# Four layers of a diffusion trunk on one core: queue order from a recorder, and one transpose for each word of q, k and P

## The chip, the core and the metric

The kernel runs on one core of a Trainium2 chip. The core has a matrix engine (TensorE, PE in the profile, with its weight loads as PEld), a vector engine (VectorE, DVE), a scalar engine (ScalarE, ACT), GpSimd (POOL) and SyncE (SP), which issues the transfers between the chip's memory and the core's SBUF. TensorE writes to PSUM, eight banks of 128 x 512 words. Each engine works through its own queue in order and waits at semaphores for the others. The metric is the device time of one execution in microseconds.

## The reference, cut to what matters

One step of a four-layer trunk over 128 context tokens and 256 latent tokens, width 2048, all in f32. Layers 0 and 3 are windowed attention (16 query heads, 4 key heads, head size 128, rotary on latents, a sink a head), layer 1 is neighbourhood attention on a 4 x 64 grid (16 heads, a relative bias), layer 2 is a gated MLP with 128 x 128 mixing of positions.

```python
for i in range(DEPTH):                       # kinds: win, nat, gmlp, win
    sh, sc, gt = split(silu(cond) @ w_ada[i] + b_ada[i])
    h = rmsnorm(x, norm_g[i]) * (1 + sc) + sh
    q, k, v, z = split(h @ w_in)             # q, k normed a head, rotary in win
    s = q @ k.T * d ** -0.5                  # own window and all context keys
    P = softmax([s + mask_or_bias, sink])    # nat: no sink
    x = x + gt * ((P @ v * silu(z)) @ w_out)
# gmlp: u, v = gelu(h @ w_in); o = u * (w_s @ layernorm(v) + b_s) * silu(z)
```

Context tokens read context tokens alone; latents read their own window or neighbourhood and 128 cached context keys. The results are the new x of both sequences and the new keys and values of the context.

## The kernel before, in words

All 384 tokens go through each layer together; x is kept transposed, 16 blocks of 128 features by 384 tokens. TensorE has no exact f32 product in one pass, so a number is split in two fp32r words, high and low (H = the rounded number, L = number - H; `split`, one ACT copy and one VectorE subtraction), and a product is three matmuls, high x high, high x low, low x high (`mm3`, `a_unit`, `b_unit`). Weights come in pieces of 128 x 1024 words (0.5 MB): SP loads one into one of four `raw` slots, `prep` splits it into one of three H and L slots, and TensorE uses it for one unit of 24 main matmuls, of 384 columns (`a_unit`, weights stationary) or 512 (`b_unit`, h stationary). `take` asks for the pieces some units ahead.

The order of every queue is written out by hand, in the order of the Python program. Between two units, `bg` advances what runs beside the projections by one step: `step_heads` (the attention heads, generators that yield where a result must come back), `step_misc` (generators for q, k, v, caches), `step_conv` (splits of the gated output) and `step_ada` (rows of the next layer's modulation on VectorE). Some of these decide by an own running count of time for TensorE, VectorE and ACT (`pe_t`, `dve_t`, `act_t`, added to in `mm`, `trR`, `_v`, `act`).

Where transposes stand: `k_gen` (four k blocks in the neighbourhood layer, one in each window layer) norms and rotates k with tokens on partitions, splits it in SBUF into two buffers pH and pL, transposes 12 blocks of 128 x 128 of each to PSUM by `trR` (line 118, fp32r words against an fp32r identity), and copies them out by `ev` (ACT or VectorE, whichever its count says is free first). `q_gen` norms and splits q of four heads likewise; `head` then transposes three blocks of each word, computes the scores, takes the maximum and exponentials into Pt, writes 1/sum x Pt as high word PH (ACT) and low word PLT (VectorE), transposes seven blocks of each word, and computes P @ v. A head so comes to TensorE for q, scores, the two words of P, and the output.

Lines of the profile are those of helpers: L109 is every matmul, L118 every transpose, L122 `tensor_tensor` on VectorE, L133 `scalar_tensor_tensor`, L129 `tensor_scalar`, L150 every ACT instruction, L142 VectorE's copies, L137 the modulation's products. So groups are told apart by their tiles: `hH`, `hL` are the words of h, `H`, `L` of a weight piece, `bk` a PSUM bank, `identR` marks the transposes, `aux,pair` the gMLP's mixing. A matmul is shown as out<-moving,stationary.

Of the kernel before, what the change touches and what calls it, by code (L numbers as in the profile page):

```python
# [1 line left out]

# [5 lines left out]
F32 = mybir.dt.float32  # L8
# [6 lines left out]
P = 128  # L15
# [21 lines left out]
    return bass.AP(ap.tensor, ap.offset, a)  # L37


class Net:  # L40
    def __init__(self, tc, pool, psum, dram, a):
        self.tc, self.nc, self.a = tc, tc.nc, a
        self.pe_t = self.dve_t = self.act_t = self.slot_t = 0.0
        self.lr = {}

# [67 lines left out]
        self.mm(out, aH, bL, False, False)  # L113
        self.mm(out, aL, bH, False, stop)

    def trR(self, out, in_):
        self.pe_t += 0.057
        self.nc.tensor.transpose(out.bitcast(F32R), in_, self.identR)  # L118

    def vtt(self, out, in0, in1, op):  # L120
        self._v(self._n(out) / 960 + 0.07)
# [311 lines left out]
    def setup(self):  # L433
        nc, a = self.nc, self.a
        self.scratch()
        craw, th = self.arow[:, :32], self.arow[:, 32:64]
        self.dma(craw, a["cT"])
        for i in range(NXP):
            self.xt[i] = self.new(f"pair{NPAIR + i}", 1536)
            self.dma(self.xt[i], a["xT"][:, i * 1536:(i + 1) * 1536])  # L440
        self.dma_upto(10)
        nc.scalar.dma_start(self.sel, a["sel"])
        self.act(th, craw, AF.Tanh, scale=0.5)
        make_identity(nc, self.ident)
# [254 lines left out]
    def k_gen(self, kind, li, grp, pi):  # L699
# [10 lines left out]
        for t in range(3):  # L710
# [14 lines left out]
                self.dma(dst[:, n:n + 512], pr[:, :512])  # L725
            else:
                yield
        hi, lo = self.palloc("x", F32R), self.palloc("x", F32R)
        pH, pL = hi[1], lo[1]
        if kind == "win":  # L730
            c3 = pr[:, :512].rearrange("p (h d) -> p h d", h=4)
            self.vtt(c3, c3, _bcast(self.gq, 1, 4), ALU.mult)
        for t in (1, 2, 0):
            o = slice(t * 512, (t + 1) * 512)
            self.split(pH[:, o], pL[:, o], pr[:, o])
        yield
        self.prel(pi)
        kH, kL = self.palloc("m", F32R), self.palloc("m", F32R)
        if kind == "win":
            self.ck = self.new("ck", 1024, F32R)  # L740
        for part, (dst, src) in enumerate(((kH, pH), (kL, pL))):
            dv = dst[1]
            for m in range(3):
                bank = self.abank()
                for i in range(4):
                    if kind == "nat":
                        h, t = divmod(m * 4 + i, 3)
                    else:
                        h, t = divmod(m * 4 + i, 2) if m < 2 else (i, -1)
                        t += 1  # L750
                    self.trR(bank[:, i * P:(i + 1) * P], src[:, t * 512 + h * P:t * 512 + h * P + P])
                if kind == "nat":
                    self.ev(dv[:, m * 512:(m + 1) * 512], bank)
                elif m < 2:
                    self.ev(dv.rearrange("p (h x) -> p h x", h=4)[:, 2 * m:2 * m + 2, :256],
                            bank.rearrange("p (h x) -> p h x", h=2))
                else:
                    self.ev(self.ck[:, part * 512:(part + 1) * 512], bank)
            yield
        self.prel(hi)  # L760
        self.prel(lo)
        grp["k"] = (kH, kL)

    def v_block(self, bk3, kind, li, grp):
# [18 lines left out]
    def q_gen(self, kind, li, grp, pi):  # L783
        pr = pi[1]
        st, st2, st3 = self.stat(), self.stat(), grp["cq"]
        yield
        self.squares(pr, st, 0, 8)
        if kind == "win":
            self.rope(pr[:, 512:1024], self.aux[:, :P], self.aux[:, 256:256 + P])
        yield  # L790
        self.squares(pr, st, 8, 12)
        if kind == "win":
            self.rope(pr[:, 1024:1536], self.aux[:, P:256], self.aux[:, 256 + P:512])
        self.vts(st2, st, P * EPS, None, ALU.add)
# [6 lines left out]
        if grp["n"] == 3:  # L801
            self.px.sort(reverse=True)
        hi, lo = self.palloc("x", F32R), self.palloc("x" if grp["n"] < 3 else "m", F32R)
        pH, pL = hi[1], lo[1]
        for t in range(3):
            o = slice(t * 512, (t + 1) * 512)
            self.split(pH[:, o], pL[:, o], pr[:, o])
        self.prel(pi)
        yield
        grp["q"] = (hi, lo)  # L810

    def head(self, kind, li, h, grp, kvg, zz):

        hh = h % 4
        kv = h // 4 if kind == "win" else hh
        qs, kT, V = ([i[1] for i in g] for g in (grp["q"], kvg["k"], kvg["v"]))
        sm = self.sm[h % 2]
        mx, nm, rs, es, rr, tt = (sm[:, 4 * i:4 * i + 3] for i in range(6))
        for part in range(2):
            bank = self.abank()  # L820
            for t in range(3):
                self.trR(bank[:, t * P:(t + 1) * P], qs[part][:, t * 512 + hh * P:t * 512 + hh * P + P])
            self.ev(self.qT[:, part * T:(part + 1) * T], bank[:, :T])
        if hh == 3:
            for i in grp["q"]:
                self.prel(i)
        yield
        b0, b1 = self.abank(), self.abank()
        k3 = [k[:, kv * T:(kv + 1) * T] for k in kT]
# [3 lines left out]
        for t, b, o in ((0, b0, P), (1, b1, 0)):  # L833
# [13 lines left out]
        Pt = self.new("Pt", 896)  # L847
# [33 lines left out]
        pt = []  # L881
        for part, src in enumerate((pH, pL)):
            b0, b1 = self.abank(), self.abank()
            for kc in range(3):
                for t in range(2):
                    o = kc * 256 + t * P
                    b, o = (b0, o) if o < 512 else (b1, o - 512)
                    s = P + t * T + kc * P
                    self.trR(b[:, o:o + P], src[:, s:s + P])
            self.trR(b1[:, 256:T], src[:, :P])  # L890
            pt.append(self.new("PLT" if part else "PTH", 896, F32R))
            self.ev(pt[part][:, :512], b0)
            self.ev(pt[part][:, 512:896], b1[:, :T])
            yield
# [486 lines left out]
    def run(self):  # L1381
# [3 lines left out]
        for l in range(4):  # L1385
# [124 lines left out]
```

## Time and profile before

| | |
|---|---|
| Median of 3 runs | 3072.14 us (3071.66 to 3074.43) |
| The profiled execution | 3072.06 us, span 3070.2 us |
| Mean granted TensorE clock | 0.998 |
| PE, PEld busy | 3032.9 us (99%), 2771.4 us (90%) |
| DVE, ACT busy | 2174.0 us (71%), 1271.6 us (41%) |
| Moved by DMA | 599 MB, mean 195 GB/s |

A busy share of PE counts matmuls from a start to a modelled end; they are pipelined, and the spans of successive ones overlap. The distance from one start to the next is the time that a matmul takes out of the stream. [...]

### The profile page before, as it was taken

Reading aid. Unit: us, or ns where it says so; the run is one execution under the profiler, and the core shown is the slowest. Engines: PE = TensorE matmul, PEld = TensorE weight load, DVE = VectorE, ACT = ScalarE, POOL = GpSimd, SP = SyncE. Lnnn points to the kernel's source line nnn. Section 1 sums busy time; section 2 is a strip of 40 time slices with the busy share of each in tenths; the row PEclk is TensorE's granted clock in tenths of the full one; section 3 lists DMA queues with packets and bytes.
Section 4 is the critical chain, followed back from the end, with each engine's and each line's share of the span. In section 5 each row is a group of like instructions: output and inputs, shape, how many; then the busy total and the mean of one; then the engine's idle time right before and its main releaser. Section 6 shows DMA issues by size and latency. Waiting matters only on the chain.

```text
span 3070.2 us, 45356 instructions
## 1 busy us (share of the span) xinstructions
PE 3032.9 (99%) x17616; PEld 2771.4 (90%) x17616; DVE 2174.0 (71%) x3604; ACT 1271.6 (41%) x2322; POOL 51.7 (2%) x29
## 2 busy tenths in 40 slices
PE   7999999999999999999999999999999999999999
PEld 4788899978989898998888999999999998999999
DVE  4478789868788888887988998445355566455654
ACT  4355555354444545534333222222232335455542
POOL 0000000000000000000000000000000000000000
PEclk9999999999999999999999999999999999999999
DMA  9756555976666666677777676444454474333343
GB/s 385 276 192 213 200 165 176 337 252 212 206 205 206 204 214 200 205 243 269 246 242 248 219 254 213 132 131 127 134 165 125 135 251 145 114 103 104 106 128 124
DMA packets 187361, 599.05 MB, mean 195 GB/s; under 512 B 21764, under 2 KB 47620, under 8 KB 187140
## 3 DMA queue, kind: packets, MB, share of 16 engines
q1 hardware_dynamic: 186712, 596.00, 58.3%
q8 instruction: 138, 2.26, 0.3%
q14 instruction: 79, 0.65, 0.1%
q10 hardware_dynamic: 432, 0.13, 0.0%
HBM read 580.31 MB, written 15.75 MB: 194 GB/s over the span
## 4 chain that ended last, share of the span: by engine, by line
PE 94%; DVE 2%; ACT 2%; issue 1%; DMA 1%; POOL 0%; SPq 0%; DVEq 0%; ACTq 0%; POOLq 0%
PE bk L109 92%; PE bk L118 3%; ACT junk L150 1%; DVE L L122 1%; DVE pair L133 1%; ACT H L150 0%; DVE pair L122 0%; POOL cq L165 0%; DMA pair<-i_w_ada 0%; ACT Pt L150 0%; DVE junk L137 0%; DMA pair<-i_xT 0%; DMA raw<-i_win_B 0%; DVE PLT L133 0%; DVE Pt L122 0%
## 5 line engine op out<-in xcount | busy, mean ns | idle before, releaser
L150 ACT ACTIVATE H<-raw 128x1024 fp32r<-128x1024 f32 x640 | 676.2, 1058 | 895.1 <-PE bk L109 805.4
L109 PE MATMUL bk<-hH,H 128*128 128x384 f32 x3072 | 1037.5, 338 | 3.4 <-DVE pair L122 3.4
L109 PE MATMUL bk<-hH,L 128*128 128x384 f32 x3072 | 1027.6, 334 | 0.0
L109 PE MATMUL bk<-hL,H 128*128 128x384 f32 x3072 | 1027.0, 334 | 0.0
L122 DVE TENSOR_TENSOR L<-raw,H 128x1024 fp32r<-128x1024 f32 x640 | 781.6, 1222 | 275.8 <-ACT H L150 267.3
L109 PE MATMUL bk<-L,hH 128*128 128x512 f32 x1536 | 600.9, 391 | 8.9 <-DVE L L122 8.9
L109 PE MATMUL bk<-H,hH 128*128 128x512 f32 x1536 | 607.5, 396 | 0.0
L109 PE MATMUL bk<-H,hL 128*128 128x512 f32 x1536 | 602.0, 392 | 0.3 <-DVE hL L122 0.3
L109 PEld LDWEIGHTS bk<-hH,H 128*128 128x128 f32 x3072 | 576.9, 188 | 13.7 <-issue 6.5
L109 PEld LDWEIGHTS bk<-hL,H 128*128 128x128 f32 x3072 | 577.1, 188 | 0.6
L109 PEld LDWEIGHTS bk<-hH,L 128*128 128x128 f32 x3072 | 576.7, 188 | 0.0
L109 PEld LDWEIGHTS bk<-L,hH 128*128 128x128 f32 x1536 | 289.5, 188 | 66.7 <-DVE L L122 11.0
L109 PEld LDWEIGHTS bk<-H,hL 128*128 128x128 f32 x1536 | 289.3, 188 | 65.3 <-DVE hL L122 3.8
L109 PEld LDWEIGHTS bk<-H,hH 128*128 128x128 f32 x1536 | 289.2, 188 | 64.6 <-issue 6.5
L137 DVE CUSTOM_DVE_ANT_0 junk<-araw,cbc,accA 128x1024 bf16<-128x1024 f32 x240 | 307.5, 1281 | 14.2 <-ACT junk L150 7.9
L137 DVE CUSTOM_DVE_ANT_0 junk<-araw,cbc,bada 128x1024 bf16<-128x1024 f32 x240 | 307.5, 1281 | 10.0 <-ACT junk L150 3.0
L133 DVE SCALAR_TENSOR_TENSOR pair<-bk,ada,pair 128x128 f32<-128x128 f32 x320 | 118.6, 413 | 202.4 <-PE bk L109 202.4
L150 ACT ACTIVATE pair<-bk 128x512 f32<-128x512 f32 (+3 forms) x156 | 86.9, 562 | 195.7 <-PE bk L109 172.4
L150 ACT ACTIVATE PLT<-bk 128x512 fp32r<-128x512 f32 (+2 forms) x63 | 34.0, 563 | 168.4 <-PE bk L118 150.2
L150 ACT ACTIVATE PTH<-bk 128x512 fp32r<-128x512 f32 (+2 forms) x74 | 37.0, 523 | 123.1 <-PE bk L118 87.9
L109 PE MATMUL bk<-pair,qT 128*128 128x384 f32 (+2 forms) x336 | 74.9, 332 | 0.0
L150 ACT ACTIVATE junk<-pair 128x128 bf16<-128x128 f32 x216 | 66.8, 309 | 13.4 <-DVE ada L137 5.9
(151 smaller groups left out, 2150.3 us busy)
## 6 DMA issues: line engine op xcount, KB each, us to landing
araw<-i_w_adaT SPq DMA_DIRECT2D x240, 512.0 KB, 3.8
pair<-i_w_ada SPq DMA_DIRECT2D x96, 512.0 KB, 8.2
raw<-i_win_B SPq DMA_DIRECT2D x96, 512.0 KB, 4.2
raw<-i_nat_B SPq DMA_DIRECT2D x96, 512.0 KB, 4.5
raw<-i_win_O SPq DMA_DIRECT2D x64, 512.0 KB, 3.7
raw<-i_gm_V SPq DMA_DIRECT2D x64, 512.0 KB, 4.6
raw<-i_gm_U SPq DMA_DIRECT2D x64, 512.0 KB, 4.5
raw<-i_gm_Z SPq DMA_DIRECT2D x64, 512.0 KB, 4.5
```

Of the source, the lines that this page charges most:

```text
L109: self.nc.tensor.matmul(out, lhsT, rhs, start=start, stop=stop, **kw)
L118: self.nc.tensor.transpose(out.bitcast(F32R), in_, self.identR)
L122: self.nc.vector.tensor_tensor(out=out, in0=in0, in1=in1, op=op)
L133: self.nc.vector.scalar_tensor_tensor(out=out, in0=in0, scalar=s, in1=in1, op0=op0, op1=op1)
L137: self.nc.vector.tensor_tensor_reduce(out=out, in0=in0, in1=in1, op0=op0, op1=op1, scale=1.0, scalar=scalar, accum_out=acc)
L150: self.nc.scalar.activation(out, in_, f, **kw)
```

## The change

Two things are changed. First, `self.nc` is no longer the chip's instruction builder but a recorder (`Rec`). The Python program runs as before and lists its instructions; `add` finds for each what it must come after (data of another instruction, or mere order on its own engine), by tile, column range and the generation of a buffer. `cost` gives each instruction a time on its engine and a time to its result. `in_order` plays the list through in program order on a model of the five queues; `due` works back from TensorE's starts to when each instruction must have started; `schedule` builds a new order, one instruction at a time: TensorE takes the earliest of the program's that is ready, with 250 ns added to results of other engines, and the other queues take what is due first. Main matmuls (those that read h) keep their order among themselves. `order` does this three times, and `emit` issues everything in order of the planned start.

Second, transposes. `trR` is replaced by `tr`, which transposes plain f32 words against the f32 identity. k, q and the scaled P are no longer split in SBUF: each is transposed once, and the split into high and low words is done out of the PSUM bank. P is scaled in place, on ACT or VectorE, and Pt has two buffers (tags Pt and PH) in turn. k's blocks go in three steps of four, with a yield behind each.

```diff
-        self.tc, self.nc, self.a = tc, tc.nc, a
+        self.tc, self.nc, self.a = tc, Rec(tc.nc), a
...
-    def trR(self, out, in_):
-        self.pe_t += 0.057
-        self.nc.tensor.transpose(out.bitcast(F32R), in_, self.identR)
+    def tr(self, out, in_):
+        self.pe_t += 0.084
+        self.nc.tensor.transpose(out, in_, self.ident)
...  k_gen
-        hi, lo = self.palloc("x", F32R), self.palloc("x", F32R)
-        pH, pL = hi[1], lo[1]
...
-        for t in (1, 2, 0):
-            o = slice(t * 512, (t + 1) * 512)
-            self.split(pH[:, o], pL[:, o], pr[:, o])
+        kH, kL = self.palloc("m", F32R), self.palloc("m", F32R)
         yield
+        dH, dL = kH[1], kL[1]
+        for m in range(3):
+            bank = self.abank()
+            for i in range(4):
...
+                self.tr(bank[:, i * P:(i + 1) * P], pr[:, t * 512 + h * P:t * 512 + h * P + P])
+            if kind == "nat":
+                o = slice(m * 512, (m + 1) * 512)
+                self.split(dH[:, o], dL[:, o], bank)
...
+            yield
...  q_gen
-        hi, lo = self.palloc("x", F32R), self.palloc("x" if grp["n"] < 3 else "m", F32R)
-        pH, pL = hi[1], lo[1]
-        for t in range(3):
-            o = slice(t * 512, (t + 1) * 512)
-            self.split(pH[:, o], pL[:, o], pr[:, o])
-        self.prel(pi)
         yield
-        grp["q"] = (hi, lo)
+        grp["q"] = pi
...  head
-        for part in range(2):
-            bank = self.abank()
-            for t in range(3):
-                self.trR(bank[:, t * P:(t + 1) * P], qs[part][:, t * 512 + hh * P:t * 512 + hh * P + P])
-            self.ev(self.qT[:, part * T:(part + 1) * T], bank[:, :T])
+        bank, pr = self.abank(), grp["q"][1]
+        for t in range(3):
+            self.tr(bank[:, t * P:(t + 1) * P], pr[:, t * 512 + hh * P:t * 512 + hh * P + P])
+        self.split(self.qT[:, :T], self.qT[:, T:], bank[:, :T])
...
-        pH, pL = self.new("PH", 896, F32R), self.new("PLT", 896, F32R)
         for t, lo, hi, _ in seg:
-            self.act(pH[:, lo:hi], Pt[:, lo:hi], AF.Identity, scale=rr[:, t:t + 1])
-            self.vstt(pL[:, lo:hi], Pt[:, lo:hi], rr[:, t:t + 1], pH[:, lo:hi].bitcast(F32), ALU.mult, ALU.subtract)
+            if self.act_t <= self.dve_t:
+                self.act(Pt[:, lo:hi], Pt[:, lo:hi], AF.Identity, scale=rr[:, t:t + 1])
+            else:
+                self.vts(Pt[:, lo:hi], Pt[:, lo:hi], rr[:, t:t + 1], None, ALU.mult)
         yield
-        for part, src in enumerate((pH, pL)):
...
+                self.tr(b[:, o:o + P], Pt[:, s:s + P])
+        self.tr(b1[:, 256:T], Pt[:, :P])
+        pt = [self.new("PTH", 896, F32R), self.new("PLT", 896, F32R)]
+        for lo, hi, b in ((0, 512, b0), (512, 896, b1[:, :T])):
+            self.split(pt[0][:, lo:hi], pt[1][:, lo:hi], b)
+        yield
...  run
+        self.nc.emit()
```

The recorder's prices and its planner, cut to their core:

```python
    def cost(self, e, op, a, k):          # ns on the engine, ns to the result
        n = self.cols(a[0] if a else k["out"])
        if e == "tensor":
            if op == "transpose":
                d = 57
            elif "tile_position" in k:
                d = 128
            elif a[2].dtype == F32R:
                d = (n + 32) / 2.4 if n > P else 57
            else:
                d = max(4 * (n + 16) / 2.4, 224)
            return d, d + 190
        if e == "vector":
...
            if op in ("tensor_tensor", "tensor_copy", "bn_stats", "tensor_reduce"):
...
                d = m / 0.96 + 72
...
            return d, d + 90
        if e == "scalar":
...
            d = n / 1.2 + 97 + (75 if hasattr(k.get("scale"), "ap") or hasattr(k.get("bias"), "ap") else 0)
...
            return d, d + 115
        if e == "gpsimd":
            return 650 + 140 * n, 750 + 140 * n
        return 330, 2100
...
    SEM, LDW, LAG = 45, 108, 56
    MARGIN = 250
...
    def schedule(self, late):
...
        key = [float(i) if self.eng[i] == 0 else late[i] for i in range(n)]
...
            i = ready[e][0][1]
            if e == 0:
                if load + self.LDW + self.LAG > t and not self.long[i]:
                    i = min((i for _, i in ready[0] if self.long[i]), default=i)
...
                load = max(load + self.LDW, last)
                t = last = max(t, load + self.LAG)
            if e in (1, 2) and wait[e]:
                end, hold = t + self.dur[i], None
                for est, j in wait[e]:
                    if est < end and late[j] < end and late[j] < late[i] and (hold is None or est < hold):
                        hold = est
                if hold is not None:
                    free[e] = hold
                    continue
...
    def order(self, passes=3):
        start, done = self.in_order()
        for _ in range(passes):
            start, done = self.schedule(self.due(start))
        return sorted(range(len(self.ops)), key=lambda i: (start[i], i))
```

`long` is an instruction of over 100 ns by `cost`, so transposes and matmuls of 128 fp32r columns are short.

## Rows read from the trace of the kernel before

**Rows 1.** The page: each engine's busy us, share, instructions; the chain that ended last.

```profile
PE 3032.9 (99%) x17616; PEld 2771.4 (90%) x17616; DVE 2174.0 (71%) x3604; ACT 1271.6 (41%) x2322; POOL 51.7 (2%) x29
...
PE 94%; DVE 2%; ACT 2%; issue 1%; DMA 1%; POOL 0%; SPq 0%; DVEq 0%; ACTq 0%; POOLq 0%
```

**Rows 2.** Timeline of TensorE, one burst: start, us, line, operation, tiles, count.

```profile
1004.36 0.39 PE L109 MATMUL bk<-L,hH 128*128 128x512 f32 x1
...
1005.27 0.39 PE L109 MATMUL bk<-H,hL 128*128 128x512 f32 x1
1005.50 0.71 PE L118 MATMUL bk<-identR,PH 128*128 128x128 f32 x7
...
1006.35 0.39 PE L109 MATMUL bk<-L,hH 128*128 128x512 f32 x1
```

**Rows 3.** Timeline of TensorE around a burst of the gMLP's mixing matmuls.

```profile
1703.83 0.33 PE L109 MATMUL bk<-hL,H 128*128 128x384 f32 x1
...
1704.52 0.34 PE L109 MATMUL bk<-hH,L 128*128 128x384 f32 x1
1704.70 0.83 PE L109 MATMUL bk<-aux,pair 128*128 128x128 f32 x6
...
1705.54 0.34 PE L109 MATMUL bk<-hL,H 128*128 128x384 f32 x1
```

**Rows 4.** Groups by shape: count; busy us, mean ns; idle time before, releaser.

```profile
L109 PE MATMUL bk<-hH,H 128*128 128x384 f32 x3072 | 1037.5, 338 | 3.4 <-DVE pair L122 3.4
...
L109 PE MATMUL bk<-H,hH 128*128 128x512 f32 x1536 | 607.5, 396 | 0.0
...
L118 PE MATMUL bk<-identR,pair 128*128 128x128 f32 x432 | 45.2, 246 | 2.0 <-DVE PTH L142 2.0
...
L118 PE MATMUL bk<-identR,PH 128*128 128x128 f32 x336 | 34.4, 243 | 0.0
```

**Rows 5.** Stretches: length; busy PE, PEld, DVE, ACT, POOL; clock; DMA; GB/s.

```profile
735.00:1420.00 685.00, 679.30 (x3849) 617.76 (x3853) 580.89 (x987) 308.13 (x608) 16.18 (x6) 1.00 0.68 220
736.00:738.00 2.00, 2.00 (x6) 1.61 (x5) 2.00 (x4) 0.30 (x1) 0.00 (x0) 0.50 0.74 250
1207.00:1209.00 2.00, 2.00 (x7) 1.51 (x6) 2.00 (x4) 0.25 (x1) 0.00 (x0) 0.50 0.70 246
8.00:17.00 9.00, 3.37 (x28) 0.55 (x32) 6.73 (x13) 6.27 (x12) 0.00 (x0) 1.00 1.02 414
```

**Rows 6.** Timeline of TensorE around a burst of k.

```profile
201.68 0.40 PE L109 MATMUL bk<-H,hL 128*128 128x512 f32 x1
201.91 1.13 PE L118 MATMUL bk<-identR,pair 128*128 128x128 f32 x12
...
203.19 0.40 PE L109 MATMUL bk<-L,hH 128*128 128x512 f32 x1
```

**Rows 7.** Timeline of TensorE at a lone short matmul.

```profile
309.32 0.22 PE L109 MATMUL bk<-mask,identR 128*128 128x128 f32 x1
...
309.79 0.33 PE L109 MATMUL bk<-hH,H 128*128 128x384 f32 x1
```

**Rows 8.** Groups by shape, of VectorE.

```profile
L122 DVE TENSOR_TENSOR L<-raw,H 128x1024 fp32r<-128x1024 f32 x640 | 781.6, 1222 | 275.8 <-ACT H L150 267.3 <-PE bk L109 4.7 <-DMA pair<-i_w_ada 3.4
...
L133 DVE SCALAR_TENSOR_TENSOR PLT<-Pt,sm,PH 128x384 fp32r<-128x384 f32 x96 | 54.8, 612 | 0.0
```

**Rows 9.** TensorE's waits: for whom, us in total, times, longest us.

```profile
PE bk L109 <- DMA pair<-i_w_ada: 13.6, 3, 13.1
PE bk L109 <- DVE L L122: 8.9, 5, 1.9
...
PE bk L109 <- DVE hL L122: 0.3, 1, 0.3
```

**Rows 10.** Timeline of all engines at one of the long waits.

```profile
888.57 3.24 DVE L133 SCALAR_TENSOR_TENSOR pair<-pair,cq,gq 128x128 f32<-128x128 f32 x12 [2.38 <-POOL cq L165]
...
893.00 0.50 PE L109 MATMUL bk<-L,hH 128*128 128x512 f32 x1 [1.90 <-DVE L L122]
```

More of the change, by code (lines that the diff above doesn't have):

```diff
@@ L1 @@
+import heapq
+import re
 from itertools import chain
@@ L443, in setup @@
         self.act(th, craw, AF.Tanh, scale=0.5)
-        make_identity(nc, self.ident)
+        make_identity(nc.real, self.ident)
         nc.vector.memset(self.ones, 1.0)
@@ L732, in k_gen @@
             self.vtt(c3, c3, _bcast(self.gq, 1, 4), ALU.mult)
-        for t in (1, 2, 0):
-            o = slice(t * 512, (t + 1) * 512)
-            self.split(pH[:, o], pL[:, o], pr[:, o])
+            self.ck = self.new("ck", 1024, F32R)
+        kH, kL = self.palloc("m", F32R), self.palloc("m", F32R)
         yield
-        self.prel(pi)
[L738 to L743, printed above, removed]
-                bank = self.abank()
[L745 to L759, printed above, removed]
@@ L760, in k_gen @@
-        self.prel(hi)
-        self.prel(lo)
+        dH, dL = kH[1], kL[1]
[3 more added lines that the diff above has]
+                if kind == "nat":
+                    h, t = divmod(m * 4 + i, 3)
+                else:
+                    h, t = divmod(m * 4 + i, 2) if m < 2 else (i, -1)
+                    t += 1
+                self.tr(bank[:, i * P:(i + 1) * P], pr[:, t * 512 + h * P:t * 512 + h * P + P])
+            if kind == "nat":
+                o = slice(m * 512, (m + 1) * 512)
+                self.split(dH[:, o], dL[:, o], bank)
+            elif m < 2:
+                part = [d.rearrange("p (h x) -> p h x", h=4)[:, 2 * m:2 * m + 2, :256] for d in (dH, dL)]
+                self.split(*part, bank.rearrange("p (h x) -> p h x", h=2))
+            else:
+                self.split(self.ck[:, :512], self.ck[:, 512:], bank)
+            yield
@@ L800, in q_gen @@
             yield
-        if grp["n"] == 3:
-            self.px.sort(reverse=True)
-        hi, lo = self.palloc("x", F32R), self.palloc("x" if grp["n"] < 3 else "m", F32R)
-        pH, pL = hi[1], lo[1]
-        for t in range(3):
-            o = slice(t * 512, (t + 1) * 512)
-            self.split(pH[:, o], pL[:, o], pr[:, o])
-        self.prel(pi)
         yield
-        grp["q"] = (hi, lo)
+        grp["q"] = pi
     def head(self, kind, li, h, grp, kvg, zz):
@@ L815, in head @@
         kv = h // 4 if kind == "win" else hh
-        qs, kT, V = ([i[1] for i in g] for g in (grp["q"], kvg["k"], kvg["v"]))
+        kT, V = ([i[1] for i in g] for g in (kvg["k"], kvg["v"]))
         sm = self.sm[h % 2]
         mx, nm, rs, es, rr, tt = (sm[:, 4 * i:4 * i + 3] for i in range(6))
-        for part in range(2):
-            bank = self.abank()
-            for t in range(3):
-                self.trR(bank[:, t * P:(t + 1) * P], qs[part][:, t * 512 + hh * P:t * 512 + hh * P + P])
-            self.ev(self.qT[:, part * T:(part + 1) * T], bank[:, :T])
+        bank, pr = self.abank(), grp["q"][1]
+        for t in range(3):
+            self.tr(bank[:, t * P:(t + 1) * P], pr[:, t * 512 + hh * P:t * 512 + hh * P + P])
+        self.split(self.qT[:, :T], self.qT[:, T:], bank[:, :T])
         if hh == 3:
-            for i in grp["q"]:
-                self.prel(i)
+            self.prel(grp["q"])
         yield
@@ L846, in head @@
                 self.mm3(b[:, o + 256:o + T], *q3(t + 1), *c3, True, True)
-        Pt = self.new("Pt", 896)
+        Pt = self.new(("Pt", "PH")[h % 2], 896)
         self.vmax(mx[:, 0:1], b0[:, :P])
@@ L875, in head @@
         yield
-        pH, pL = self.new("PH", 896, F32R), self.new("PLT", 896, F32R)
         for t, lo, hi, _ in seg:
-            self.act(pH[:, lo:hi], Pt[:, lo:hi], AF.Identity, scale=rr[:, t:t + 1])
-            self.vstt(pL[:, lo:hi], Pt[:, lo:hi], rr[:, t:t + 1], pH[:, lo:hi].bitcast(F32), ALU.mult, ALU.subtract)
+            if self.act_t <= self.dve_t:
+                self.act(Pt[:, lo:hi], Pt[:, lo:hi], AF.Identity, scale=rr[:, t:t + 1])
+            else:
+                self.vts(Pt[:, lo:hi], Pt[:, lo:hi], rr[:, t:t + 1], None, ALU.mult)
         yield
-        pt = []
-        for part, src in enumerate((pH, pL)):
[L883 to L894, printed above, removed]
+        b0, b1 = self.abank(), self.abank()
+        for kc in range(3):
+            for t in range(2):
+                o = kc * 256 + t * P
+                b, o = (b0, o) if o < 512 else (b1, o - 512)
+                s = P + t * T + kc * P
+                self.tr(b[:, o:o + P], Pt[:, s:s + P])
[4 more added lines that the diff above has]
+        yield
         bank = self.abank()
```

201 lines of the change are left out of this document (added).

## The prediction

> **What bounds the kernel now.** I read the busy table first, then the chain of waits, then TensorE's groups by shape, then the stretches in which TensorE stood still. TensorE is busy 99% of the span, and the chain that ends last runs on it for 94% [rows 1]. Busy spans overlap there, so the reader should count from start to start instead. In an undisturbed stream a 512-column matmul starts 0.227 us after the one before ((1005.27 - 1004.36)/4), a 384-column one 0.173 us after ((1704.52 - 1703.83)/4) [rows 2, 3]. The main projections are 3 x 3072 matmuls of 384 columns and 3 x 1536 of 512, three to a product [rows 4]: 9216 x 0.1733 + 4608 x 0.2267 = 2642 us, 86% of the span of 3070.2 us. The rest of TensorE's time is small matmuls and transposes in bursts between them, and a little standing still. VectorE has 71%, ScalarE 41% [rows 1]; in the neighbourhood layer VectorE comes to 580.9 of 685 us, and TensorE has 679.3 all the same [rows 5]. So a microsecond taken out of TensorE's stream should come off the end almost one for one, and one taken from VectorE or ScalarE only where TensorE waited for it.
>
> **The change part by part.**
>
> *Transposes.* Before, there are 432 of q and k and 336 of P's high words, and as many low ones [rows 4]: 1104, in 48 heads with 6 for q and two bursts of 7 for P, and 12 bursts of 12 for k. After, it is half: 552, in 48 x 3, 48 x 7 and 18 x 4. What one costs is read from the bursts. Around a burst of 7, from the start of the last main matmul before it to that of the second one behind it, 1006.35 - 1005.27 = 1.08 us pass; less 2 x 0.227 that is 0.626 us [rows 2]. A burst of 12: 203.19 - 201.68, less 0.453, is 1.057 us [rows 6]. The slope is (1.057 - 0.626)/5 = 0.086 us a transpose, the rest 0.024 us a burst. Before: 48 x 0.540 + 96 x 0.626 + 12 x 1.057 = 98.7 us. After, in whole bursts: 48 x 0.282 + 48 x 0.626 + 18 x 0.368 = 50.2 us.
>
> The recorder prefers a long matmul where the next weight load isn't ready, so it breaks bursts up, into pairs as I read its rule. A lone short matmul among long ones takes, from 309.32 to 309.79 and less two of 0.173, 0.12 us [rows 7]: more than in a burst. By 0.086n + 0.024 a pair costs 0.196, so 276 pairs 54.1 us; all 552 alone at 0.11 to 0.12 cost 61 to 66 us. The saving is 48.5 (whole), 44.6 (pairs) or 33 to 38 us (alone). I take 46, between whole and pairs, since P's seven become ready together.
>
> [...]
>
> *Words of plain f32.* All 1104 now move fp32r words; after the change they are f32. No row shows an f32 transpose. From below I bound it by the price of now, 0.086 us. From above by the gMLP mixing matmul, f32 at the same 128x128: a burst of six records, which is three matmuls in the code, takes 1705.54 - 1704.52 - 0.347 = 0.673 us [rows 3], so 0.224 us each. 552 x 0.224 = 124 us, 25 more than now. I take 0.086: the present ones are one record each and are shown as f32 in the profile too, and a transpose has no product that would need a second pass.
>
> [...]
>
> *Splits and evacuations.* Before, q and k are split in SBUF (54 pairs of instructions on 512 columns), and each scaled P is written as a high word on ACT and a low word on DVE (144 pairs; 96 of them take DVE 54.8 us, 0.612 each [rows 8]). These go, and P is scaled once in place, on ACT or on DVE; either is priced at the same 0.612 us, for no row scales in place. Out of PSUM it was two copies, on either engine; now one copy on ACT and one subtraction on DVE: as many instructions. Saved, as an estimate from that row: 54 x 0.6 = 32 us of ACT and (54 + 144) x 0.6 = 120 us of DVE over the whole run. TensorE's stream hides nearly all of it today, so I count nothing beyond the waits below. The new cost is order: copy and subtraction run one behind the other ahead of a head's scores and of its output product, where two copies could run side by side, 0.6 us more each time. Main matmuls stand in between and hide it; if they did not, it would be 48 x 2 x 0.6 = 58 us. I take none of it, and keep half for the range.
>
> *The recorder.* It lists every instruction and DMA with what it needs, works out when TensorE will want each, and issues all queues in the order of that plan. The order among the main matmuls stays; what moves is where the small ones stand, and everything on VectorE, ScalarE and the DMA queue. What can go is standing still: TensorE's nine rows of waits come to 33.6 us, 13.1 of them for the first weights [rows 9]; 20.5 remain. 8.9 of these are five waits for the low words of weights, the longest 1.9 us, and the one shown (three others look the same) has this cause: VectorE scales q for 3.24 us before it makes the low words of the next weights, and TensorE gets these late [rows 10]. An order by due time puts the weights first, and the q split behind it is gone. [...] So up to 20.5 + 2 = 22.5 us can go. I take 17: the weight waits with their clock, and half of the rest. On the other side are new waits, where the plan is wrong. Its prices agree with the rows (main 173 and 227 ns, weight split on DVE 1.23 us to the result against 1.222 [rows 8]); only a lone short matmul it holds for 57 ns. I take +3 us.
>
> *DMA queue.* Transfers that wait for a free weight slot hold those behind them in SP's queue; an order by due time changes which. In the neighbourhood layer the DMA share is 0.68 [rows 5], so a transfer that is moved by some us is covered by the slots ahead; only where it is full is there no cover, at the start: 414 GB/s at a share of 1.02 from 8 to 17 us [rows 5]. The first matmul waits 13.1 us there, for its weights to land [rows 9]. Six weight transfers more or less ahead of x gain up to 5 us there, or lose as much (0.5 MB at 414 GB/s is 1.3 us each; estimate). I take -2.
>
> **Sum.** The profiled execution took 3072.06 us, its span 3070.2; the median of the three timed runs is 3072.14, so both are one. -46 -17 +3 -2 = -62: 3010 us.
>
> **Rivals.** *Only the transposes pay*: the stalls move elsewhere, because TensorE waits for data and not for order. 3072 - 46 = 3026. For it: a plan can only move the 0.7% of the span that these waits are. Against it: the largest group of them has a cause that the change touches.
>
> *f32 transposes take two passes*: +25 in place of -46, the recorder's -16 stays: 3081 us, slower. For it: f32 matmuls cost 0.224 us here. Against it: one record each, as above.
>
> *The plan's order is wrong on the chip*: each head comes to TensorE four times (q, scores, P, output), 192 visits, and the plan leaves 0.25 us between a result and the matmul that reads it; TensorE takes its matmuls in order, so every late result holds the main stream. From a mean wait of 46/192 = 0.24 us the transposes' gain is gone; at half a weight split on VectorE in front of each result (1.222/2 = 0.61 us) it is 117 us, so 3072 - 46 + 117 = 3143 us. For it: VectorE is 85% busy in the neighbourhood layer. Against it: the plan's prices fit, and VectorE loses 120 us of work.
>
> **How the numbers follow.** Forecast 0.66, only the transposes 0.20, two passes 0.06, wrong order 0.08 (some of it at small waits, near no change). The forecast's own range is 2997 to 3022. The low end takes every gain: 48.5 + 22.5 + 5 = 76, so 2996, and I go 5 lower, to 2991, for weight loads that hide better than the lone row shows. The high end takes transposes alone (-38 to -33), no stall gained and half of the serial copy (+29): 3062 to 3068, and I stop at 3062. About 0.2% (6 us) is what a measurement of this kernel can tell from no change. Faster: 0.66 + 0.20 = 0.86; the same 0.04; slower 0.10.
>
> **What would show it.** 552 transposes, one record each, 84 to 90 ns apart in a burst: the price is right; 1104 records or gaps over 0.2 us: two passes. No 2 us wait at the neighbourhood layer's groups and no clock of 0.50 behind: the recorder's part is right. TensorE's waits after the start at 20 us or more: only the transposes paid, or the order is wrong. If the main matmuls are no longer 173 and 227 ns apart, my base was wrong.

## The result, and the profile after

The changed kernel takes 3051.14 us (median of 4 runs, 3048.99 to 3052.81) against 3071.92 us for the kernel before on the same chip: a ratio of 0.993, 95% interval 0.9913 to 0.9947, so 20.8 us less. The forecast was 62 us less. The sign came out; two thirds of the size did not. The time lies inside the wide range (2991 to 3062 us) and outside the forecast's own (2997 to 3022).

The page of the kernel after, busy times and chain of waits, against [rows 1]:

```profile
PE 3005.5 (99%) x17064; PEld 2733.9 (90%) x17064; DVE 2085.1 (68%) x3499; ACT 1202.4 (39%) x2175; POOL 59.0 (2%) x29
...
PE 87%; DVE 5%; DMA 5%; issue 2%; ACT 1%; SPq 0%; DVEq 0%; ACTq 0%
```

TensorE has 552 instructions fewer and 27 us less busy time. But its share of the chain fell from 94% to 87%: the end now hangs on VectorE and on transfers for 10%, where it was 3%.

TensorE's groups by shape, to be held against [rows 4] (count; busy us, mean ns; idle before). All of them are at L314, the line on which the recorder issues:

```profile
L314 PE MATMUL bk<-hH,H 128*128 128x384 f32 x3072 | 1040.4, 339 | 3.6 <-DVE pair L314 3.6
...
L314 PE MATMUL bk<-ident,pair 128*128 128x128 f32 x216 | 45.5, 274 | 0.0
L314 PE MATMUL bk<-ident,Pt 128*128 128x128 f32 x168 | 34.0, 272 | 0.0
L314 PE MATMUL bk<-ident,PH 128*128 128x128 f32 x168 | 34.0, 272 | 0.0
```

216 + 168 + 168 = 552, one record each, so the rival of two passes falls. Of what one costs in the stream the timeline tells more, against the burst in [rows 6]:

```profile
200.56 0.39 PE L314 MATMUL bk<-H,hL 128*128 128x512 f32 x1
200.79 0.38 PE L314 MATMUL bk<-ident,pair 128*128 128x128 f32 x2
200.93 0.48 PE L314 MATMUL bk<-H,hH 128*128 128x512 f32 x1
201.24 0.38 PE L314 MATMUL bk<-ident,pair 128*128 128x128 f32 x2
201.38 0.48 PE L314 MATMUL bk<-L,hH 128*128 128x512 f32 x1
201.69 0.40 PE L314 MATMUL bk<-H,hL 128*128 128x512 f32 x1
```

The transposes stand in pairs, as forecast. From 200.56 to 201.69 there are three main matmuls and two pairs: 1.13 - 3 x 0.227 = 0.449 us, 0.225 a pair, 0.112 a transpose. At this price all 552 cost 62 us (an estimate), against 98.7 before: 37 us saved, not 46.

TensorE's waits after, against [rows 9] (for whom; us in total, times, longest):

```profile
PE bk L314 <- DVE spad L314: 11.3, 1, 11.3
PE bk L314 <- DVE pair L314: 8.4, 7, 2.9
PE bk L314 <- DVE sm L314: 6.9, 18, 1.3
PE bk L314 <- ACT hH L314: 3.8, 4, 1.7
PE bk L314 <- DMA pair<-i_w_ada: 2.0, 1, 2.0
PE bk L314 <- DVE L L314: 1.9, 4, 0.7
```

The waits for low words of weights did fall, from 8.9 to 1.9 us, and the longest from 1.9 to 0.7: what the prediction read at [rows 10] is gone. But the whole list comes to 37.7 us, where it was 33.6; without the wait at the start, 26.4 where it was 20.5. A new row, `sm`, has 18 waits, and two more, in rows not shown, are for `qT`.

VectorE's own waits show the other new thing (before, the trace has 4.8 us in 6 waits for `araw`, and no row for `cbc`):

```profile
DVE junk L314 <- DMA araw<-i_w_adaT: 36.2, 40, 3.4
DVE junk L314 <- DMA cbc<-srow: 17.4, 12, 2.9
```

The stretches of [rows 5] (length; busy PE, PEld, DVE, ACT, POOL; clock; DMA share; GB/s), with the two places where the clock falls now:

```profile
735.00:1420.00 685.00, 678.51 (x3749) 611.68 (x3749) 599.21 (x1048) 294.92 (x582) 20.33 (x7) 1.00 0.75 238
1217.00:1219.00 2.00, 2.00 (x10) 2.00 (x10) 2.00 (x4) 0.00 (x0) 0.00 (x0) 0.50 0.78 195
1691.00:1693.00 2.00, 2.00 (x7) 1.90 (x8) 2.00 (x4) 0.00 (x0) 0.00 (x0) 0.50 0.64 166
8.00:17.00 9.00, 3.53 (x27) 1.03 (x27) 6.76 (x15) 6.00 (x14) 0.00 (x0) 1.00 1.03 422
```

The stalls at 736 and 1207 us no longer cost their clock, but the stretch from 1216.4 us (6.8 us long, after waits of 0.90 and 1.25 us for `qT` and `sm`) and the one from 1690.8 us (3.4 us, after a wait of 2.86 us for the gMLP's norm) are at a granted clock of 0.50. From 1219.83 to 1222.71 us a matmul of 384 columns starts every 0.320 us there, where it takes 0.173 at 1.00, so near half of such a stretch is lost (an estimate from these distances). Not every such wait has that behind it: after 1.70 us for `hH` at 643.3 us and 1.51 us at 239.2 us the clock stays at 1.00. At the low clock of 0.50 there were 13.7 us before, start included, and 10.2 us after. The start is nearly what it was: the first matmul comes after 11.3 us in place of 13.1, the first main matmul at 29.1 us in place of 30.8.

What makes TensorE wait for `sm`, all engines at one of the 18 places:

```profile
389.68 0.39 PE L314 MATMUL bk<-pair,qT 128*128 128x384 f32 x1
...
390.11 0.29 DVE L314 TENSOR_REDUCE sm<-bk 128x1 f32<-128x128 f32 x1 [0.72 <-PE bk L314]
390.31 1.28 DVE L314 CUSTOM_DVE_ANT_0 junk<-araw,cbc,accA 128x1024 bf16<-128x1024 f32 x1
...
390.45 0.44 PE L314 MATMUL bk<-pair,qT 128*128 128x384 f32 x1 [0.38 <-DVE sm L314]
```

A head's scores are written to a bank in several matmuls, and VectorE takes the maximum over the first 128 columns. The recorder notes PSUM by columns, so it plans that maximum between two matmuls into the same bank; here the next matmul stands for 0.38 us and starts at 390.45 us, when VectorE's read (0.29 us from 390.11) is over. Where the maximum itself stands behind a modulation product of 1.28 us, the wait is 1.25 us (1216.68 us).

And what VectorE's waits for transfers do, in the neighbourhood layer's adjoining modulation:

```profile
1398.37 0.60 PE L314 MATMUL bk<-ck,sT 128*2 128x256 f32 x4
...
1398.58 1.28 DVE L314 CUSTOM_DVE_ANT_0 junk<-araw,cbc,bada 128x1024 bf16<-128x1024 f32 x1 [2.09 <-DMA araw<-i_w_adaT]
...
1399.79 0.67 DVE L314 TENSOR_SCALAR PH<-ident,st 128x128 f32<-128x128 f32 x3
...
1400.12 0.71 PE L314 MATMUL bk<-PH,ones 128*128 128x128 f32 x4 [1.15 <-DVE PH L314]
```

A product that could have come later holds VectorE for 2.09 us until its rows of weights land, and the norm's step behind it, for which TensorE waits 1.15 us, comes late.

### The profile page after: what moved, and what is told of

Its sections match the earlier page's. It is cut to its first block, busy times and chain, and to the rows that moved or that the text cites. A ratio compares the mean times of both kernels' runs of the same rounds, so it can differ in the third digit from the quotient of the medians.

```text
span 3047.2 us, 44052 instructions
## 1 busy us (share of the span) xinstructions
PE 3005.5 (99%) x17064; PEld 2733.9 (90%) x17064; DVE 2085.1 (68%) x3499; ACT 1202.4 (39%) x2175; POOL 59.0 (2%) x29
## 4 chain that ended last, share of the span: by engine, by line
PE 87%; DVE 5%; DMA 5%; issue 2%; ACT 1%; SPq 0%; DVEq 0%; ACTq 0%
PE bk L314 87%; DMA araw<-i_w_adaT 3%; DVE junk L314 2%; DVE L L314 2%; DMA raw<-i_win_B 0%; DVE pair L314 0%; DMA cbc<-srow 0%; DVE bn L314 0%; DMA pair<-i_xT 0%; DVE sm L314 0%; ACT Pt L314 0%; DVE Pt L314 0%; ACT H L314 0%; DMA pair<-i_masks 0%; DMA sel<-i_sel 0%
## 5 line engine op out<-in xcount | busy, mean ns | idle before, releaser
L314 ACT ACTIVATE H<-raw 128x1024 fp32r<-128x1024 f32 x640 | 678.2, 1060 | 1498.8 <-PE bk L314 1378.4
L314 DVE TENSOR_TENSOR L<-raw,H 128x1024 fp32r<-128x1024 f32 x640 | 782.4, 1223 | 447.3 <-ACT H L314 445.6
L314 PE MATMUL bk<-hH,H 128*128 128x384 f32 x3072 | 1040.4, 339 | 3.6 <-DVE pair L314 3.6
L314 PE MATMUL bk<-hL,H 128*128 128x384 f32 x3072 | 1034.0, 337 | 0.0
L314 PE MATMUL bk<-hH,L 128*128 128x384 f32 x3072 | 1031.5, 336 | 0.7 <-DVE L L314 0.7
L314 PE MATMUL bk<-H,hH 128*128 128x512 f32 x1536 | 607.7, 396 | 5.7 <-ACT hH L314 3.8
L314 PE MATMUL bk<-L,hH 128*128 128x512 f32 x1536 | 605.4, 394 | 1.4 <-DVE L L314 1.2
L314 PE MATMUL bk<-H,hL 128*128 128x512 f32 x1536 | 601.9, 392 | 0.0
L314 PEld LDWEIGHTS bk<-hH,H 128*128 128x128 f32 x3072 | 578.1, 188 | 14.1 <-DVE pair L314 5.0
L314 PEld LDWEIGHTS bk<-hH,L 128*128 128x128 f32 x3072 | 577.7, 188 | 1.5 <-DVE L L314 1.0
L314 PEld LDWEIGHTS bk<-hL,H 128*128 128x128 f32 x3072 | 578.1, 188 | 1.0
L314 PEld LDWEIGHTS bk<-H,hH 128*128 128x128 f32 x1536 | 288.6, 188 | 68.9 <-issue 5.7
L314 PEld LDWEIGHTS bk<-L,hH 128*128 128x128 f32 x1536 | 288.6, 188 | 61.0 <-DVE L L314 4.4
L314 PEld LDWEIGHTS bk<-H,hL 128*128 128x128 f32 x1536 | 288.5, 188 | 58.0 <-issue 0.4
L314 DVE CUSTOM_DVE_ANT_0 junk<-araw,cbc,accA 128x1024 bf16<-128x1024 f32 x240 | 307.4, 1281 | 38.7 <-DMA araw<-i_w_adaT 19.3
L314 DVE CUSTOM_DVE_ANT_0 junk<-araw,cbc,bada 128x1024 bf16<-128x1024 f32 x240 | 307.4, 1281 | 18.8 <-DMA araw<-i_w_adaT 16.9
L314 DVE SCALAR_TENSOR_TENSOR pair<-bk,ada,pair 128x256 f32<-128x256 f32 x320 | 119.4, 413 | 213.2 <-PE bk L314 212.0
L314 ACT ACTIVATE pair<-bk 128x512 f32<-128x512 f32 (+3 forms) x162 | 89.5, 555 | 59.4 <-PE bk L314 57.8
L314 PE MATMUL bk<-pair,qT 128*128 128x384 f32 (+2 forms) x336 | 86.0, 343 | 5.2 <-DVE sm L314 4.3
L314 DVE TENSOR_TENSOR pair<-pair,aux 128x512 f32<-128x512 f32 (+1 forms) x108 | 59.8, 589 | 18.8 <-ACT pair L314 15.5
L314 ACT ACTIVATE PTH<-bk 128x512 fp32r<-128x512 f32 (+1 forms) x112 | 54.0, 514 | 40.3 <-PE bk L314 39.8
L314 ACT ACTIVATE junk<-pair 128x128 bf16<-128x128 f32 x216 | 66.5, 308 | 6.0 <-DVE accA L314 1.4
```

The source lines that it names most:

```text
L314: getattr(getattr(self.real, e), op)(*a, **k)
```

## The experiments

Two halves of the change, each alone; then the recorder's plan amended in the two ways that the traces suggest; then the prices. Each median stands against the kernel before on the same chip (3071.95 to 3072.55 us throughout).

**The new transposes alone.** The recorder is taken out; the program's own order runs.

```diff
-        self.tc, self.nc, self.a = tc, Rec(tc.nc), a
+        self.tc, self.nc, self.a = tc, tc.nc, a
...
-        self.nc.emit()
```

> The new transposes alone, in the queue order written by hand; no recorder. The trace of the changed kernel shows an isolated pair of f32 transposes at 0.225 us, 0.112 each. Theory A: an f32 transpose costs 0.112 us wherever it stands; 552 of them with 114 bursts at 0.024 are 65 us against 98.7 before, so -34: about 3038 us, and the recorder then cost some 13 us. Theory B: f32 words cost what fp32r words cost in a whole burst (0.086), only the recorder's pairs made them dear: -48, about 3023 us, and the recorder cost 28. Theory C: the transposes gave only the 21 us that the change brought, the recorder nothing: 3051 us.

Measured: 3075.47 us, ratio 1.0013 (1.0003 to 1.0022). None of the theories had it: some 37 us of transposes were saved and more than lost again. TensorE's waits come to 61.3 us in place of 33.6, and 41.0 us are at the low clock in place of 13.7, which costs half of the 27.3 more: 27.7 + 13.6 - 36.6 (98.7 less 276 x 0.225) = +4.7 us, against +3.5 measured. The rows that grew, and three of the stretches that they lie in (columns as in [rows 5]):

```profile
PE bk L386 <- DVE PLT L400: 6.4, 4, 5.0
PE bk L386 <- DVE pair L411: 6.0, 1, 6.0
PE bk L396 <- ACT PH L428: 5.7, 2, 3.0
PE bk L396 <- DVE Pt L405: 4.2, 2, 2.9
```

```profile
318.00:322.00 4.00, 1.18 (x6) 0.63 (x4) 0.00 (x0) 0.00 (x0) 0.00 (x0) 1.00 1.00 364
1274.00:1292.00 18.00, 8.35 (x40) 7.78 (x41) 9.29 (x21) 5.37 (x14) 0.00 (x0) 0.70 0.17 58
480.00:492.00 12.00, 8.54 (x51) 7.82 (x52) 7.73 (x20) 5.29 (x14) 0.00 (x0) 0.89 0.00 1
```

At 318 us everything stands for a load of weights (the DMA share is 1.00). The trace shows what it stood behind: SP, which takes its queue in order, held a load of modulation rows until VectorE had read the buffer it goes to (its product ends at 312.4 us), and the load of weights stands behind it in the queue:

```profile
312.49 0.33 SPq L379 DMA_DIRECT2D araw<-i_w_adaT  x1
...
313.81 0.43 SPq L379 DMA_DIRECT2D raw<-i_win_B  x1
...
322.34 1.06 ACT L428 ACTIVATE H<-raw 128x1024 fp32r<-128x1024 f32 x1 [10.25 <-DMA raw<-i_win_B]
```

In the other two the program's order puts no main matmul between a head's steps, from 477.2 to 494.1 us and from 1272.3 to 1291.8 us:

```profile
477.18 0.49 PE L396 MATMUL bk<-ident,pair 128*128 128x128 f32 x3
...
479.87 0.94 DVE L405 TENSOR_SCALAR Pt<-Pt,sm 128x128 f32<-128x128 f32 x3
...
480.54 1.20 PE L396 MATMUL bk<-ident,Pt 128*128 128x128 f32 x7 [2.87 <-DVE Pt L405]
...
481.45 0.98 ACT L428 ACTIVATE PTH<-bk 128x512 fp32r<-128x512 f32 x2 [2.45 <-PE bk L396]
...
482.08 1.16 DVE L400 TENSOR_TENSOR PLT<-bk,PTH 128x512 fp32r<-128x512 f32 x2 [0.81 <-ACT PTH L428]
```

Scaling, transposes, copy and subtraction run there one behind the other, the serial order that the prediction took as hidden. In the kernel before TensorE does not stand still from 470 to 500 us nor from 1260 to 1300.

**The recorder alone**, over the old kernel's split and its 1104 transposes of fp32r words.

```diff
-        self.tc, self.nc, self.a = tc, tc.nc, a
+        self.tc, self.nc, self.a = tc, Rec(tc.nc), a
...
+        self.nc.emit()
```

> The recorder alone, over the kernel before with its 1104 fp32r transposes and its splits in SBUF. Theory A (the recorder adds waits of its own, above all TensorE behind a VectorE maximum that is moved between the matmuls of one bank): pairs of fp32r transposes 0.196 in place of 0.172 each two, +10, and waits +10 to +15: 3080 to 3097 us. Rival (the recorder gains by itself what I forecast, and the loss lies with the transposes): 3072 - 14 + 10 = 3068 or less.

Measured: 3092.32 us, 1.0065 (1.005 to 1.008): slower, as theory A had it. TensorE's waits are 33.0 us, no less than before, 5.8 of them for `sm` and 7.6 for `pair`; VectorE waits 38.7 us for the modulation's rows (`araw`). So each half alone loses, and both together gain.

**Whole banks.** In `span`, any touch of a PSUM tile counts as one of its whole bank.

```diff
+        if name[:2] == "bk":
+            return name, 0, 512, ap.tensor.name
         lo = int(ap.offset) % max(p[0][0], 1)
```

> The changed kernel, with the recorder told that every access to a PSUM bank touches the whole bank, so that a maximum over a bank's first columns is planned behind all matmuls into that bank. Theory A: the 19 waits of TensorE's weight loads for the maxima (11.3 us, VectorE sm) go, perhaps with the half clock of 6.8 us behind the longest (3.4 us): 3051 - 11 to -15, 3036 to 3040 us. Rival (those waits only move to the next thing that is late): 3048 to 3053 us.

Measured: 3041.66 us, 0.9904 (0.9888 to 0.9921), 9.5 us under the changed kernel, between the two expectations and nearer to theory A; no row for `sm` is left among TensorE's waits. Its listed waits fell only from 37.7 to 32.9 us, and 17.0 us are at the low clock in place of 10.2, so waits and clock explain 4.8 - 3.4 = 1.4 of the 9.5; where the rest was saved is not shown. A plan by columns can't know of a wait like the 0.38 us at 390.45 us.

**Old kernel, transposes of f32 words.** Same count and order as before, only the word's type changed.

```diff
-        self.nc.tensor.transpose(out.bitcast(F32R), in_, self.identR)
+        self.nc.tensor.transpose(out, in_.bitcast(F32), self.ident)
```

> The kernel before, its 1104 transposes as plain f32 words against the f32 identity, in whole bursts as before; nothing else changed. Theory A (an f32 transpose costs 0.112 us in a burst too): 1104 x 0.112 + 156 x 0.024 = 127 against 98.7, +28: 3100 us. Theory B (same price as fp32r, 0.086): 3072 us, no change. Two passes at 0.224: +150, 3220 us.

Measured: 3089.88 us, 1.0059 (1.0044 to 1.0074), between theories A and B and far from two passes. The burst of 7, to be held against [rows 2]:

```profile
1014.86 0.39 PE L109 MATMUL bk<-H,hL 128*128 128x512 f32 x1
1015.09 0.93 PE L118 MATMUL bk<-ident,PH 128*128 128x128 f32 x7
...
1016.08 0.39 PE L109 MATMUL bk<-L,hH 128*128 128x512 f32 x1
```

1016.08 - 1014.86 - 0.453 = 0.767 us, where the fp32r words took 0.626. A burst of 12 takes 1.327 (203.23 to 205.01 us), so the slope is 0.112 in place of 0.086. By these bursts 1104 would cost 22 us more; 17.8 came, with TensorE's waits 2.2 us shorter (31.4) and 6.8 us less at the low clock (6.8 in place of 13.7), worth 5.6 us together.

**Landing 2 us later.** On top of whole banks, a transfer's data are planned for 3300 ns after the model's end of the transfer.

```diff
-                done[i] = max(dma + 1300, t + self.lat[i])
+                done[i] = max(dma + 3300, t + self.lat[i])
```

> The whole-bank version (3041.7 us), with the recorder holding a transfer for landed 2 us later than before (3.3 in place of 1.3 us behind the modelled queue). In the changed kernel VectorE waits 36.2 us for the modulation's rows, 40 times, before the change 4.8 us; it takes its queue in order, so what TensorE needs stands behind. Theory A: with later landings planned, these waits fall below 10 us and TensorE's with them: 3030 to 3036 us. Rival (VectorE's waits for these rows fill time that it had to spare): 3039 to 3044 us.

Measured: 3022.76 us, 0.9837 (0.9822 to 0.9852): 18.9 us under whole banks alone, more than theory A had. It beats both kernels and is the fastest of all. VectorE's waits and the first rows of TensorE's:

```profile
DVE junk L316 <- DMA araw<-i_w_adaT: 12.7, 16, 1.7
DVE junk L316 <- DMA cbc<-srow: 3.3, 5, 0.8
```

```profile
PE bk L316 <- DVE spad L316: 11.0, 1, 11.0
PE bk L316 <- DVE pair L316: 3.9, 5, 1.3
```

VectorE's waits for transfers, 53.6 us in the changed kernel and 46.0 with whole banks alone, became 16.0. TensorE's waits are 22.6 us in place of 37.7 and 32.9, and one stretch of 3.4 us at the low clock is left, where whole banks alone had 17.0. Against whole banks alone that is 10.3 us of waits and 6.8 of clock, 17.1 of the 18.9.

**More margin in place of it.** On top of whole banks, results of other engines are planned 1500 ns late for TensorE, not 250.

> The whole-bank version (3041.7 us), with 1500 ns in place of 250 ns planned between another engine's result and the TensorE instruction that reads it. Theory A (the plan leaves TensorE too little slack, main matmuls could stand in between): TensorE's waits behind VectorE and ACT after the start fall from about 20 us to under 10, with the half clock behind them: 3028 to 3036 us. Rival (banks and buffers are held longer, heads fall behind and end up without main matmuls beside them at a layer's end): 3042 to 3055 us.

Measured: 3057.46 us, 0.9951 (0.9935 to 0.9968): 15.8 us slower than whole banks, 2.5 us beyond the rival's window. TensorE's waits are 41.7 us in place of 32.9, and 34.0 us are at the low clock in place of 17.0, 8.8 and 8.5 us. Time in hand for every result alike does not help at 1500 ns (other margins were not run).

**Bursts left whole**, first for the new transposes with whole banks, then for the old ones under the recorder as it was.

```diff
-        self.long.append(d > 100)
+        self.long.append(d > 100 or op == "transpose")
```

> The whole-bank version (3041.7 us), with transposes planned in whole bursts in place of pairs among main matmuls. An f32 transpose took 0.110 us in a burst and 0.112 in an isolated pair. Theory A (for f32 words pairs cost nothing more): 3040 to 3043 us. Rival (the breaking up itself costs 0.01 to 0.02 us for each of 552): 3030 to 3036 us.

Measured: 3042.03 us (3035.89 to 3049.12), 0.99 (0.9883 to 0.9917): no difference that can be told from the pairs' 3041.66, with some 5 us of noise. For f32 words a pair alone costs 2 x 0.112, as in a burst.

> The recorder over the kernel before (3092.3 us), with its 1104 fp32r transposes planned in whole bursts. There an isolated pair costs 0.204 us, 0.102 each, against 0.086 to 0.090 in a burst. Theory A (breaking up fp32r bursts is most of what the recorder loses there): -13, 3077 to 3081 us. Rival (the loss is in waits): 3088 to 3094 us.

Measured: 3083.65 us, 1.0031 (1.0018 to 1.0045): 8.7 us less than cut into pairs, between the two theories. fp32r words do pay for the cutting. In the recorder's order with pairs (the run of the recorder alone) six pairs and seven main matmuls stand between these starts:

```profile
200.57 0.40 PE L314 MATMUL bk<-H,hL 128*128 128x512 f32 x1
200.80 0.28 PE L314 MATMUL bk<-identR,pair 128*128 128x128 f32 x2
...
203.38 0.39 PE L314 MATMUL bk<-H,hH 128*128 128x512 f32 x1
```

(2.81 - 7 x 0.227)/6 = 0.204 us a pair, 0.102 each, against 98.7/1104 = 0.089 in the bursts.

**The later landing alone**, without whole banks.

> The changed kernel with the recorder's landing time put 2 us later (3300 ns after the transfer's end in the model, in place of 1300), PSUM still noted by columns. Theory A, two separate gaps in the plan, each with its price: the 19 us that the later landing gave on top of whole banks come off the changed kernel's 3051 alone, 3030 to 3035, VectorE's waits for the modulation rows fall from 36 us to about 13, and the waits for the maximum over a half bank stay near 7 us. Rival, the two need each other (VectorE's late work is hidden behind the waits on half banks): 3038 to 3048.

Measured: 3033.21 us, 0.987 (0.9856 to 0.9883), 17.9 us under the changed kernel, in theory A's window. `sm` keeps 6.0 us in 16 waits and `araw` falls to 10.7 us. So the two gaps are separate and add up: whole banks are worth 9.5 us without the later landing and 10.5 with it, the later landing 17.9 without whole banks and 18.9 with them.

**The recorder with both amendments over the old transposes**, then the same with their bursts whole.

> The recorder over the old kernel's transposes of high and low parts, with both amendments of the plan (whole banks, landing 2 us later); it ran at 3092 without them. Theory A: the amendments are worth what they were worth in the changed kernel, 9.5 and 19 us, so 3060 to 3068, which would put the recorder's own term at some 4 to 12 us of gain against the kernel before, and the transposes' at 37 to 45 under it. Rival, VectorE has less left to wait for where the parts are split before the transposes, and the cut-up pairs of short transposes are the whole loss: 3072 to 3085.

Measured: 3069.41 us, 0.999 (0.9981 to 0.9999), just above theory A's window.

> The recorder over the old kernel's transposes with both amendments of the plan (3069.4 in the run before), and its bursts of transposes left whole. Theory A: what still ate the recorder's gain there is the cutting of the bursts into pairs, 1104 x (0.102 - 0.089) = 14 us at most and 8.7 as it was measured on the recorder's plan without the amendments, so 3055 to 3061, and the recorder's term of the forecast (17 us of stalls) is there, 11 to 17 us, when nothing cuts the bursts. Rival, whole bursts leave VectorE and ScalarE behind, so that waits come back for what the bursts save: 3066 to 3072.

Measured: 3055.11 us, 0.9943 (0.9929 to 0.9957), at the low end of theory A. The recorder's order, planned with whole banks and the later landing and not cutting the bursts, gains 16.9 us over the old order with the old transposes. TensorE's waits are 20.4 us in place of 33.6, and 3.4 us are at the low clock in place of 13.7: 13.2 + 5.1 = 18.3 us. The longest of the waits:

```profile
PE bk L316 <- DVE spad L316: 11.2, 1, 11.2
```

**Landing 4 us later** (`dma + 5300`), with whole banks.

> Whole banks and the landing 4 us later (5300 ns). Theory A: the rows of modulation land some 2 us after the model's time, so that the 2 us of the run before have closed the gap: 3019 to 3026, the same as its 3022.8. Rival 1, the queue's transfers are still later than planned in places: 3008 to 3018, with the last VectorE waits for them gone. Rival 2, a landing planned too late holds back work that could go: over 3028.

Measured: 3039.32 us, 0.9891 (0.9878 to 0.9905): rival 2, 16.6 us slower than with 2 us. VectorE's waits for rows fall to 7.7 us, but 15.3 us are lost in one place, at a layer's boundary (17.0 us at the low clock lie about it):

```profile
1390.56 0.61 PE L316 MATMUL bk<-sel,PTH 128*128 128x4 f32 x4 [0.56 <-ACT PTH L316]
1406.48 0.79 PE L316 MATMUL bk<-H,hH 128*128 128x512 f32 x1 [15.31 <-ACT hH L316]
```

In between VectorE makes eight of the modulation products that the next layer's norm needs, two of them after waits of 2.16 and 1.24 us for their rows: they came too late, though each transfer was allowed more; how the plan came to that was not followed. 2 us is the best of the three values run; others were not.

All of it in one table (us; a dash was not run):

| transposes | program's order | recorder as changed | with whole banks | and landing +2 us |
|---|---|---|---|---|
| old, bursts whole | 3072 | 3083.7 | - | 3055.1 |
| old, cut up by the planner | - | 3092.3 | - | 3069.4 |
| new, bursts whole | 3075.5 | - | 3042.0 | - |
| new, cut up by the planner | - | 3051.1 | 3041.7 | 3022.8 |

## Why the prediction came out too large

The forecast was short by 41 us, and the table splits it: 16.9 us gained by a recorder that plans right, 32.3 by the transposes from there (3055.1 to 3022.8), 28.4 lost to the plan's two gaps (3022.8 to 3051.1): -16.9 - 32.3 + 28.4 = -20.8. The split goes by one path through the table; by another the parts would be of another size.

- *The step that failed first: "Its prices agree with the rows", and with it "+3" for new waits, where 28.4 us came.* I compared matmuls and VectorE's instructions with the trace and left out two things of the recorder's model. It lets PSUM be shared by columns: 9.5 us. And it has 0.5 MB land 700 + 524288/395 + 1300 = 3327 ns after the issue, where the page of the kernel after has 4.5 us in the median for `araw`: 17.9 to 18.9 us. The page before had 3.8 us for the same rows and 3.7 to 4.6 for pieces of weights, so the second gap could have been seen before the run. Beside the bytes the model has 2.0 us, and the trace, with its 4.5, about 3.2 (an estimate: 4.5 less 1.3 for 0.5 MB at the 414 GB/s of [rows 5]; a median can hold some waiting behind other transfers).
- *Transposes, -46.* Half the count and the pairs were right, the price was not: 0.112 and not 0.086 us, since an f32 word is not the fp32r word that [rows 2, 6] show. I bounded it by 0.086 and 0.224 and took the lower end because of the records' look; the truth lay between, near that end. By the price 37 us, by the table 32; of the 4 us between them 2.2 are waits of TensorE (22.6 against 20.4), the rest is not placed. That 37 falls near the 33 to 38 us reckoned for transposes that stand alone is chance: they stood in pairs, and the word was dearer. In the bursts f32 words cost 0.026 us a transpose more than fp32r words (0.112 against 0.086). The 5 us by which the low end of the wide range goes below the gains, for weight loads that hide better than the lone row, are shown by no run: in pairs an f32 transpose took 0.112 us and an fp32r one 0.102, against that row's 0.12.
- *Serial copy and subtraction, 0.* Wrong in the order that the term was argued from: in the program's order some heads' steps stood bare, which is part of the 41 us that ate the transposes' gain there. The recorder's amended order hides nearly all of it, as the table's last column shows. The two halves are not a sum of two terms: the new transposes are worth +3.5 us in the old order and -46.6 in the amended recorder's against the same planner with the old ones. That this comes close to the forecast's 46 is chance: the new words cost more than was forecast (0.112), and the old ones, being cut up there, do too (0.102).
- *The recorder, -17.* Right in size and cause only once its plan is right: 16.9 us with the old bursts whole. In the changed kernel the weight waits did fall, from 8.9 to 1.9 us, but others took their place. The half clock behind each of the two stalls of [rows 5] lasts 3.4 us in the trace and so costs about 1.7 us, where the sum's 2 us had 1.0 for each, read from a stretch of 2 us. The cutting of bursts, priced at 3.9 us (48.5 less 44.6), costs f32 words nothing that can be measured and fp32r words 8.7 to 14.3 us.
- *Start, -2.* Right: 13.1 became 11.3 us.
- *The rival of the wrong order* named the mechanism that came, results later than the plan has them, and priced it at 117 us. It came at a quarter of that. Its sign of recognition, 20 us or more of waits after the start, is there, 37.7 - 11.3 = 26.4 us; but it tells little, since the kernel before had 20.5.
- *The rival "only the transposes pay"*, 3026 us, did not come: the time is 25 us above it.

What is left open: TensorE's waits and its clock account for some 18 us of the 28.4 (15.1 of waits, 3.4 of half clock); where the other 10 lie is not shown.

## What to carry to other kernels

A planner's order is only as good as its model, so check every price in it against the trace before you count its gain: the landing of transfers (17.9 to 18.9 us here) and the order of instructions on one PSUM bank (9.5 us), not only the engines' instructions. An instruction that waits for a late transfer, as VectorE's product did for 2.09 us at 1398.58 us, holds what stands behind it in its queue, and here that cost more than the stalls listed on the engine that matters: the later landing alone gained 17.9 us here, while TensorE's listed waits fell by 10.0 (37.7 to 27.7). Two edits that meet in the same order should be forecast together, each in the order that the other makes.

## What was not expected of the hardware

- A 128x128 transpose of f32 words cost 0.112 us in a burst and 0.225 a pair alone; of fp32r words 0.086 in a burst and 0.204 a pair. The f32 matmul of that size took 0.224 [rows 3].
- Standing still cost more than the wait itself in two places of the changed kernel: after waits of 0.90 and 1.25 us within 3 us, TensorE ran 6.8 us at the granted clock of 0.50; after one of 2.86 us, 3.4 us. After one of 1.70 us it ran on at 1.00.
